# Two transformer blocks on one core: compressor MLP in column groups, squares on ScalarE, adds to GpSimd, a new planned order

## The chip, the core and the metric

The kernel runs on one core of a Trainium2 chip. The core has TensorE (PE, with its weight loads as PEld), VectorE (DVE), ScalarE (ACT), GpSimd (POOL) and SyncE (SP), which issues the transfers. The metric is the device time of one execution in microseconds (us).

## The reference, cut to what matters

All data is float32, one sequence of 512 tokens, 1024 features. Two blocks follow each other; the second has two layers, and most of the changed code lies there.

```python
def compress(t, j):                       # second block, sparse attention: 31 windows of 32 tokens
    z = (t[:, blk] + cmp_pos[j]).reshape(B, n_cmp, CMP_BLOCK * HD)   # 31 x 2048
    return jax.nn.silu(z @ cmp_w1[j]) @ cmp_w2[j]                    # 2048 x 128, then 128 x 64

# linear attention, per head of 32 key features, chunks of 64 tokens
att = jnp.einsum('bhntd,bhnsd->bhnts', q * jnp.exp(b - b_mid), k * jnp.exp(b_mid - b))

for l in range(DEPTH):
    mod = cond @ w_mod[l] + b_mod[l]                    # six modulation vectors a layer
    ...
    x = x + gt1 * rms_norm(y, norm_g[l, 1])
    h = rms_norm(x, norm_g[l, 2]) * (1.0 + sc2) + sh2
    y = jnp.square(jax.nn.relu(h @ w_up[l])) @ w_down[l]   # 1024 -> 4096 -> 1024
    x = x + gt2 * rms_norm(y, norm_g[l, 3])
```

## The kernel before

Activations lie feature by feature on the 128 partitions. Every large product is made of three float32r products: a tensor is split into a rounded part `hi` (a copy on ScalarE) and a rest `lo` (a subtraction on VectorE), and `mm3` multiplies hi by hi, hi by lo and lo by hi. Weights come in blocks of 128x1024 (`raw`), are split into `wh`, and feed PE. From its third block of columns on, the up projection of the MLP is done by a scheme with seven products in place of eight (`winograd_fm`); its sums and differences of weight blocks are the tiles `w`.

The code writes no order. Each call on an engine is recorded in a `Plan`, with a cost in us and the buffers it touches. `schedule` then simulates the engines and picks, step by step, the ready instruction that can start first, and among those the one with the highest priority; the priority comes from due times counted backwards along PE's work and from a table `SCHED` by phase of the program (`bias` shifts a phase's priority, `wins` says how far ahead of the oldest open instruction a phase may take buffers). The resulting order is fixed in the program. Every instruction is emitted from one line (553 before, 558 after), so all rows of the profile carry that line, and instructions are told apart by their tiles: `pg` are the work tiles, `sa` and `sb` small columns, `ps` the PSUM banks, `xT` the residual, `mc` the modulation columns.

An addition written as `G.tensor_tensor` (G is GpSimd) is recorded for VectorE, and may be moved to GpSimd when `other[1] * fill <= free`: `other[1]` is its cost there, `free` the VectorE work that the planner sees at hand which does not need the second SBUF read path. With `fill = 1e9` none is moved. `op.port` marks the instructions that need that path: a GpSimd operation, or a VectorE one with two SBUF inputs.

The places touched: `mod_cols` makes eight of the 128 modulation sums of a row at a time; `attn_half` and `nsa_chain` hold the two softmax attentions; `nsa_chain` also holds the compressor MLP, whose 32 products a layer have 31 columns of weights each; `gla_chain` the linear attention; `ev_up` and `ev_quarter` the squared ReLU. At three places, which I call **crossings**, one product ends, the residual is normed, and the next product starts on the normed residual: `Sandwich.sums` and `Sandwich.apply`, whose inner loop is

```python
V.tensor_mul(self.gy[k][:, sl], self.gy[k][:, sl], bc1[:, :256])
G.tensor_tensor(xT[k][:, sl], xT[k][:, sl], self.gy[k][:, sl], op=OP.add)
```

followed by `make_h`, which reads `xT`. Each crossing does it for two halves of 256 tokens, eight tiles each.

Of the kernel before, what the change touches and what calls it, by code (L numbers as in the profile page):

```python
# [10 lines left out]
F32 = mybir.dt.float32  # L11
# [20 lines left out]
    ahead=3.0, alap=1.0, lead={'mods': 20}, near=0.0, rate=270000.0, stretch=1.0, slack={"pg": 4, "w4": 0},  # L32
    wins={
# [117 lines left out]
class Plan:  # L151
# [15 lines left out]
    rate = 3.1e5  # L167
    lead = {}
    share = True
    fill = 1e9  # L170

    def __init__(self, nc, pools, win=6000, slack=None, fifo=(), **kw):
        self.__dict__.update(kw)
# [2391 lines left out]
```

## Time and profile before

| | |
|---|---|
| median of 3 runs | 1946.89 us (1945.47 to 1948.85) |
| profiled execution, its own time | 1957.53 us |
| its span, first to last instruction | 1955.6 us |
| PE busy | 1878.0 us |
| DVE busy | 1651.0 us |
| ACT busy | 986.9 us |
| POOL busy | 12.6 us |
| mean granted clock of PE | 0.967 |

The profiled execution is 10.6 us longer than the median of the runs. Busy time of PE counts every matmul to its modelled end, so a busy PE can still have small gaps. A granted clock of 1.00 is 2.4 GHz, 0.50 is 1.2 GHz; a value between them is a mean over a stretch.

### The profile page before, as it was taken

To read this page: it belongs to the slowest core of one execution; us is meant where nothing else is said; L and a number is where in the kernel's file an instruction comes from. 1 tells how busy PE (TensorE), PEld (TensorE's weight loads), DVE (VectorE), ACT (ScalarE), POOL (GpSimd) and SP (SyncE) were. 2 spreads that over 40 slices of the span, in tenths; PEclk is the share of its full clock that TensorE was granted. 3 is DMA by queue.
4 is the path that set the end of the run, shared out by engine and by line. 5 is a ranking of instruction groups with operands and counts; after the bars stand their busy time and mean duration, and the time that the engine had idled before them with its cause. 6 is when DMAs were issued, how large, how long until landed. Compare 5 with 4: busy or idle time off the path is not lost.

```text
span 1955.6 us, 33131 instructions
## 1 busy us (share of the span) xinstructions
PE 1878.0 (96%) x12451; PEld 1680.7 (86%) x12451; DVE 1651.0 (84%) x3712; ACT 986.9 (50%) x1958; POOL 12.6 (1%) x29
## 2 busy tenths in 40 slices
PE   8889999999999999999889999989999989999998
PEld 3789887998898988778778899988987889999998
DVE  6978898897996879877999877797966789887777
ACT  4756675544334556545554444355753447433344
POOL 0000000000000000000000000001000000000000
PEclk9999999999999999979999999989998789999999
DMA  8633533337433156211245422414521023332221
GB/s 274 223 111 135 178 123 115 120 126 264 150 112 110 59 192 198 73 33 65 98 162 201 144 97 98 153 49 180 185 106 44 33 76 109 119 108 87 98 98 66
DMA packets 88240, 243.17 MB, mean 124 GB/s; under 512 B 10059, under 2 KB 27247, under 8 KB 87824
## 3 DMA queue, kind: packets, MB, share of 16 engines
q1 hardware_dynamic: 88080, 241.05, 36.3%
q8 instruction: 98, 1.61, 0.3%
q14 instruction: 62, 0.51, 0.1%
HBM read 232.63 MB, written 8.39 MB: 123 GB/s over the span
## 4 chain that ended last, share of the span: by engine, by line
PE 80%; DVE 16%; ACT 2%; issue 1%; DMA 1%; SPq 0%; DVEq 0%; ACTq 0%
PE ps L553 80%; DVE pg L553 10%; DVE sa L553 2%; ACT pg L553 1%; DVE wh L553 1%; DVE mraw L553 1%; DVE xT L553 1%; SPq L553 0%; DVE w L553 0%; ACT wh L553 0%; DMA pg<-in_hy_w_dram 0%; DMA gq<-in_k_norm_g_dram 0%; DMA kf<-pg 0%; DVE sb L553 0%; ACT mraw L553 0%
## 5 line engine op out<-in xcount | busy, mean ns | idle before, releaser
L553 PE MATMUL ps<-pg,wh 128*128 128x256 f32 (+1 forms) x6336 | 1102.3, 330 | 15.8 <-DVE pg L553 8.7
L553 PEld LDWEIGHTS ps<-pg,wh 128*128 128x128 f32 x6336 | 926.6, 191 | 122.7 <-issue 10.8
L553 PE MATMUL ps<-wh,pg 128*128 128x256 f32 (+2 forms) x2976 | 386.7, 285 | 9.8 <-ACT pg L553 5.2
L553 DVE TENSOR_TENSOR pg<-pg 128x256 f32<-128x256 f32 (+4 forms) x757 | 361.0, 512 | 32.4 <-ACT pg L553 19.2
L553 PEld LDWEIGHTS ps<-wh,pg 128*128 128x128 f32 x2976 | 370.1, 191 | 14.9 <-ACT pg L553 9.7
L553 ACT ACTIVATE wh<-raw 128x1024 fp32r<-128x1024 f32 (+3 forms) x280 | 257.8, 924 | 217.9 <-PE ps L553 209.9
L553 DVE TENSOR_TENSOR wh<-raw,wh 128x1024 fp32r<-128x1024 f32 (+3 forms) x280 | 294.1, 1053 | 66.8 <-ACT wh L553 51.8
L553 ACT ACTIVATE pg<-pg 128x256 fp32r<-128x256 f32 (+5 forms) x424 | 201.9, 500 | 201.9 <-DVE pg L553 159.9
L553 PE MATMUL ps<-pg 128*128 128x256 f32 (+9 forms) x1776 | 285.9, 311 | 14.1 <-DVE pg L553 6.0
L553 PEld LDWEIGHTS ps<-pg 128*128 128x128 f32 (+5 forms) x1776 | 240.6, 194 | 51.3 <-issue 13.9
L553 DVE TENSOR_TENSOR pg<-pg,ps 128x256 f32<-128x256 f32 (+1 forms) x428 | 192.8, 465 | 42.2 <-PE ps L553 33.2
L553 DVE TENSOR_TENSOR pg<-ps,pg 128x512 f32<-128x512 f32 (+7 forms) x274 | 146.2, 566 | 32.0 <-ACT pg L553 18.4
L553 ACT ACTIVATE pg<-ps 128x512 fp32r<-128x512 f32 (+5 forms) x214 | 106.2, 521 | 121.4 <-PE ps L553 104.3
L553 ACT COPY pg<-ps 128x256 f32<-128x256 f32 (+4 forms) x188 | 81.2, 449 | 107.6 <-PE ps L553 79.9
L553 ACT ACTIVATE wh<-w 128x512 fp32r<-128x512 f32 x112 | 70.2, 630 | 122.5 <-PE ps L553 67.8
L553 DVE TENSOR_TENSOR wh<-w,wh 128x512 fp32r<-128x512 f32 x112 | 76.9, 686 | 30.3 <-PE ps L553 18.1
L553 DVE CUSTOM_DVE_ANT_0 mraw<-mraw,crow 128x1024 f32<-128x1024 f32 x72 | 87.4, 1220 | 7.6 <-DMA mraw<-in_wmT_dram 7.6
L553 PE MATMUL ps<-ident,pg 128*128 128x128 f32 (+1 forms) x513 | 84.9, 279 | 4.6 <-DVE pg L553 3.7
L553 ACT ACTIVATE mraw<-mraw 128x1024 f32<-128x1024 f32 x56 | 59.3, 1060 | 55.4 <-DVE mraw L553 55.2
L553 PEld LDWEIGHTS ps<-ident,pg 128*128 128x128 f32 (+1 forms) x513 | 62.4, 144 | 16.2 <-DVE pg L553 3.5
L553 ACT ACTIVATE pg<-ps,sa 128x512 f32<-128x512 f32 (+3 forms) x112 | 60.3, 549 | 27.1 <-DVE sa L553 23.6
L553 DVE TENSOR_TENSOR mraw<-mraw,crow 128x1024 f32<-128x1024 f32 x56 | 68.0, 1219 | 0.8 <-DMA mraw<-in_wmT_dram 0.8
(135 smaller groups left out, 1144.4 us busy)
## 6 DMA issues: line engine op xcount, KB each, us to landing
mraw<-in_wmT_dram SPq DMA_DIRECT2D x128, 512.0 KB, 4.1
raw<-in_w_up_dram SPq DMA_DIRECT2D x64, 512.0 KB, 3.2
raw<-in_w_down_dram SPq DMA_DIRECT2D x64, 512.0 KB, 3.3
raw<-in_w_in_dram SPq DMA_DIRECT2D x32, 512.0 KB, 4.1
raw<-in_od_w_in_dram SPq DMA_DIRECT2D x28, 512.0 KB, 3.4
raw<-in_ev_w_in_dram SPq DMA_DIRECT2D x20, 512.0 KB, 3.5
raw<-in_w_dram SPq DMA_DIRECT2D x16, 512.0 KB, 5.0
raw<-in_w_o_dram SPq DMA_DIRECT2D x16, 512.0 KB, 3.2
```

What stands on the lines that cost most here:

```text
L553: o.fn(*[r(v) for v in o.args], **{k: r(v) for k, v in o.kw.items()})
```

## The change

Seven edits. The compressor MLP's products go to four groups of 32 columns of the PE array (two for each of keys and values), and the halves are added afterwards. The linear attention's products alternate between two heads. The squared ReLU is a Relu and two Squares on ScalarE, where one Square writes the rounded part. The modulation sums are all done by the fused VectorE operation. One of two softmax scalings goes to ScalarE. `fill` becomes 0.5, the port rule looks at the inputs by position, and the table `SCHED` has new numbers (two lines stand for it).

```diff
-        "L0 gemm 0": -8, "L0 gemm 2": -8, "L0norm": -100, "L0out": -207, "L0q": 151, "L1 gemm 0": 145,
+        "": -15, "L0 gemm 0": -8, "L0 gemm 2": -8, "L0norm": 20, "L0out": -215, "L0q": 106, "L1 gemm 0": 145,
...
+    fill=0.5, ahead=3.0, near=0.0,
...
-        big = [v for v in ins if max(v.shape[1:], default=1) > 1]
+        big = [v for v in list(a)[0 if "out" in k else 1:] + [v for n, v in k.items() if n not in ("out", "accum_out")]
+               if isinstance(v, View) and max(v.shape[1:], default=1) > 1]
...
+                if not f:
+                    op.cost *= 0.25 if w == 31 else 0.5 if a[1].shape[0] <= 64 else 0.7 if w == 64 else 1.0
...
-            if t in ((1, 2, 4, 5, 7) if i < 4 else (2, 5, 7)):
-                G.tensor_tensor(raw, raw, crow, op=OP.mult)
-                A.activation(raw, raw, AF.Copy, accum_out=dst[:, t:t + 1])
-            else:
-                V.tensor_tensor_reduce(raw, raw, crow, 1.0, 0.0, OP.mult, OP.add, accum_out=dst[:, t:t + 1])
+            V.tensor_tensor_reduce(raw, raw, crow, 1.0, 0.0, OP.mult, OP.add, accum_out=dst[:, t:t + 1])
...
-            V.tensor_scalar(pr, pr, rz, None, op0=OP.mult)
+            A.activation(pr, pr, AF.Copy, scale=rz)
...
+        for q in range(4):
+            wq = [pg(), pg()]
+            for j in range(2):
+                D_(wq[j], a["cmp_w1_2"][l, j, q])
+            for i0 in (0, 2):
+                for j in range(2):
+                    zv = zst[j].rearrange("p (b n e) -> p b n e", b=2, n=32)
+                    for i in (i0, i0 + 1):
+                        g = 32 * (2 * j + i - i0)
+                        ab, pe = divmod(q * 4 + i, 8)
+                        T.matmul(ph[g:g + 31, 0:P], zv[:, ab, ab:ab + 31, pe], wq[j][:, i * P:(i + 1) * P],
+                                 start=(q + i0 == 0), stop=(q == 3 and i0 == 2), tile_position=(0, g),
+                                 skip_group_check=True)
+        yield
+        hs, hb = pg(), hp()
         for j in range(2):
...
+            A.copy(hb[0:31, j * P:j * P + P], ph[64 * j + 32:64 * j + 63, 0:P])
+            V.tensor_add(hs[0:31, j * P:j * P + P], ph[64 * j:64 * j + 31, 0:P], hb[0:31, j * P:j * P + P])
+        A.activation(hs[0:31, 0:256], hs[0:31, 0:256], AF.Silu)
...
-                        for b in range(2):
-                            V.tensor_scalar(pt[b], pt[b], rz[:, b:b + 1], None, op0=OP.mult)
+                        V.tensor_scalar(pt[0], pt[0], rz[:, 0:1], None, op0=OP.mult)
+                        A.activation(pt[1], pt[1], AF.Copy, scale=rz[:, 1:2])
...
-            for h in (2 * pr, 2 * pr + 1):
-                ps = axt()
-                for tt in range(4):
+            heads = {h: axt() for h in (2 * pr, 2 * pr + 1)}
+            for tt in range(4):
+                for h, ps in heads.items():
...
         def ev_up(m, ps):
-            r, f = pg(), pg()
+            r, f, hi, lo = pg(), pg(), pg(F32R), pg(F32R)
             A.activation(r, ps, AF.Relu)
-            V.tensor_mul(f, r, ps)
-            hid.append(split(f, eng=G))
+            A.activation(f, r, AF.Square)
+            A.activation(hi, r, AF.Square)
+            V.tensor_sub(lo, f, hi.bitcast(F32))
+            hid.append((hi, lo))
...
-                            V.scalar_tensor_tensor(f, src, 0.0, src, op0=OP.max, op1=OP.mult)
-                        split(f, eng=G, hi=tiles[m][0][:, sl], lo=tiles[m][1][:, sl])
+                        A.activation(r, src, AF.Relu)
+                        A.activation(hi, r, AF.Square)
+                        A.activation(f, r, AF.Square)
+                        V.tensor_sub(lo, f, hi.bitcast(F32))
```

What the planner makes of it, at three places. The first is PE at the compressor of the second block's first layer (31x128 are its products, `wh` x 272 those of the linear attention's projection, `ident` transposes). Before:

```order
L553 MATMUL ps<-wh_377,pg 128x272
L553 MATMUL ps<-pg 31x128
L553 MATMUL ps<-ident,pg 128x128 x4
L553 MATMUL ps<-pg 31x128 x5
L553 MATMUL ps<-ident,pg 128x128 x4
L553 MATMUL ps<-pg 31x128 x17
L553 MATMUL ps<-ident,pg 128x128 x4
L553 MATMUL ps<-pg 31x128 x3
L553 MATMUL ps<-ident,pg 128x128 x4
L553 MATMUL ps<-pg 31x128 x6
L553 MATMUL ps<-wh_375,pg 128x272
```

After:

```order
L558 MATMUL ps<-wh_378,pg 128x272
L558 MATMUL ps<-wh_377,pg 128x272
L558 MATMUL ps<-pg 31x128 x32
L558 MATMUL ps<-wh_375,pg 128x272
L558 MATMUL ps<-wh_376,pg 128x272
```

The 32 products stand in one piece, and the transposes between them went elsewhere.

The second is VectorE in the first half of the first crossing, where the projection `w_o` ends and the MLP begins (`mc_409` are the modulation columns). Before:

```order
L553 SCALAR_TENSOR_TENSOR sa<-sa 128x2
L553 SCALAR_TENSOR_TENSOR pg<-ps,mc_409,xT 128x256
L553 TENSOR_TENSOR pg<-pg,ps 128x256 x2
L553 TENSOR_TENSOR xT<-xT,pg 128x256
L553 TENSOR_TENSOR pg<-pg,ps 128x256
L553 TENSOR_TENSOR xT<-xT,pg 128x256
L553 TENSOR_TENSOR pg<-pg,ps 128x256
L553 SCALAR_TENSOR_TENSOR pg<-xT,mc_409,ps 128x256
```

After:

```order
L558 SCALAR_TENSOR_TENSOR sa<-sa 128x2
L558 TENSOR_TENSOR pg<-pg,ps 128x256 x4
L558 SCALAR_TENSOR_TENSOR pg<-xT,mc_409,ps 128x256
L558 TENSOR_TENSOR pg<-pg,ps 128x256
L558 SCALAR_TENSOR_TENSOR pg<-xT,mc_409,ps 128x256
L558 TENSOR_TENSOR pg<-pg,ps 128x256
L558 SCALAR_TENSOR_TENSOR pg<-xT,mc_409,ps 128x256
```

The additions into `xT` are gone from VectorE. They stand on GpSimd, which before has only copies and memsets in this part of the program; after, its rows here are (the rows ahead of the first `xT` belong to the chains before the crossing, the `xT` rows to its two halves):

```order
L558 COPY pg<-pg 128x4x64 x8
L558 TENSOR_TENSOR pg<-pg,msk 128x256 x5
L558 TENSOR_TENSOR pg<-pg 128x512 x8
L558 TENSOR_TENSOR pg<-pg 128x256 x2
L558 TENSOR_TENSOR xT<-xT,pg 128x256 x8
L558 TENSOR_TENSOR pg<-pg 128x256
L558 TENSOR_TENSOR xT<-xT,pg 128x256 x7
```

Of the 16 additions of this crossing, 15 moved to GpSimd. The third place is ScalarE in the up projection of the first layer's MLP (`wh<-raw` and `wh<-w` are splits of weights, `pg<-pg 128x256` the squared ReLU and its split, `mraw` a modulation sum). Before:

```order
L553 ACTIVATE wh_373<-raw_370 128x1024
L553 ACTIVATE pg<-ps 128x256
L553 ACTIVATE wh_375<-raw_368 128x1024
L553 ACTIVATE pg<-pg 128x256
L553 ACTIVATE mraw_380,m_1_402<-mraw_380 128x1024
L553 ACTIVATE wh_377<-raw_369 128x1024
L553 ACTIVATE pg<-pg 128x256
```

After:

```order
L558 ACTIVATE wh_373<-raw_370 128x1024
L558 ACTIVATE pg<-ps 128x256
L558 ACTIVATE wh_375<-raw_368 128x1024
L558 ACTIVATE pg<-pg 128x256 x2
L558 ACTIVATE wh_377<-raw_369 128x1024
L558 ACTIVATE pg<-pg 128x256 x6
```

Between the same weight splits stand eight squares and ReLUs where two stood, and no modulation sum.

## Rows read from the trace of the kernel before

**Rows 1.** The page, busy time of PE and DVE: us, share, instructions.
```profile
PE 1878.0 (96%) x12451; PEld 1680.7 (86%) x12451; DVE 1651.0 (84%) x3712; ACT 986.9 (50%) x1958; POOL 12.6 (1%) x29
```

**Rows 2.** Windows by stage: stretch, length, busy of each engine, granted clock, DMA share, GB/s.
```profile
0.00:150.00 150.00, 129.15 (x791) 96.71 (x792) 119.23 (x294) 87.76 (x190) 0.77 (x10) 0.95 0.62 198
...
232.00:312.00 80.00, 74.00 (x442) 63.77 (x440) 77.12 (x169) 52.11 (x123) 0.00 (x0) 0.98 0.40 138
...
830.00:885.00 55.00, 54.70 (x291) 43.02 (x291) 41.32 (x102) 22.32 (x43) 0.00 (x0) 0.81 0.12 39
885.00:960.00 75.00, 65.06 (x444) 60.20 (x443) 65.58 (x185) 40.54 (x80) 0.00 (x0) 0.93 0.21 71
960.00:1060.00 100.00, 92.78 (x573) 82.85 (x572) 98.43 (x181) 53.21 (x95) 0.00 (x0) 0.95 0.50 169
...
1290.00:1335.00 45.00, 33.94 (x208) 31.64 (x207) 44.50 (x153) 25.45 (x61) 0.00 (x0) 0.77 0.17 58
...
1500.00:1535.00 35.00, 35.00 (x157) 28.62 (x157) 19.98 (x56) 7.17 (x13) 0.00 (x0) 0.61 0.04 16
1535.00:1608.00 73.00, 65.05 (x402) 58.05 (x401) 64.09 (x176) 33.98 (x65) 0.00 (x0) 0.88 0.20 70
1608.00:1915.00 307.00, 307.00 (x2605) 307.00 (x2605) 257.92 (x525) 137.66 (x257) 0.00 (x0) 1.00 0.29 101
1915.00:1955.60 40.60, 31.62 (x273) 31.41 (x271) 31.11 (x104) 18.62 (x56) 0.00 (x0) 0.93 0.18 66
```

**Rows 3.** The chain that ended last, in the second crossing, 1290 to 1335 us.
```profile
by line: DVE pg L553 48.1%; PE ps L553 13.7%; DVE xT L553 10.2%; DVE sa L553 9.5%; DVE wh L553 7.8%; ACT pg L553 5.5%; issue 4.9%; DVE sb L553 1.2%; DVEq L553 0.0%
```

**Rows 4.** Groups on PE by form: count, busy us, mean ns, idle before.
```profile
L553 PE MATMUL ps<-pg 128*31 128x128 f32 x128 | 16.4, 277 | 0.0
...
L553 PE MATMUL ps<-pg 32*128 32x128 f32 x64 | 9.5, 327 | 0.0
```

**Rows 5.** Timeline of PE from 720 us: start, length, matmul records.
```profile
720.66 0.31 PE L553 MATMUL ps<-sb,pg 128*64 128x31 f32 x4
720.90 0.32 PE L553 MATMUL ps<-pg,sb 128*31 128x64 f32 x8
```

**Rows 6.** Groups on VectorE by form.
```profile
L553 DVE TENSOR_TENSOR pg<-pg,ps 128x256 f32<-128x256 f32 x344 | 136.5, 413 | 30.2 <-PE ps L553 23.5 <-ACT pg L553 6.6
L553 DVE TENSOR_TENSOR pg<-pg 128x512 f32<-128x512 f32 x159 | 105.8, 683 | 4.3 <-ACT pg L553 3.2 <-DMA kf<-pg 0.8
...
L553 DVE CUSTOM_DVE_ANT_0 mraw<-mraw,crow 128x1024 f32<-128x1024 f32 x72 | 87.4, 1220 | 7.6 <-DMA mraw<-in_wmT_dram 7.6
...
L553 DVE TENSOR_TENSOR mraw<-mraw,crow 128x1024 f32<-128x1024 f32 x56 | 68.0, 1219 | 0.8 <-DMA mraw<-in_wmT_dram 0.8
...
L553 DVE SCALAR_TENSOR_TENSOR pg<-pg 128x256 f32<-128x256 f32 x90 | 36.5, 418 | 0.8
...
L553 DVE TENSOR_TENSOR xT<-xT,pg 128x256 f32<-128x256 f32 x48 | 19.8, 414 | 0.0
...
L553 DVE TENSOR_SCALAR pg<-pg,sa 128x512 f32<-128x512 f32 x40 | 18.7, 479 | 0.7
```

**Rows 7.** Groups on ScalarE by form.
```profile
L553 ACT ACTIVATE mraw<-mraw 128x1024 f32<-128x1024 f32 x56 | 59.3, 1060 | 55.4 <-DVE mraw L553 55.2
...
L553 ACT ACTIVATE pg<-pg 128x256 f32<-128x256 f32 x74 | 29.4, 413 | 25.6 <-DVE pg L553 19.3 <-DVE sa L553 5.9
...
L553 ACT ACTIVATE pg<-pg,sa 128x256 f32<-128x256 f32 x7 | 3.2, 497 | 2.2 <-DVE sa L553 2.2
```

**Rows 8.** Timeline of POOL from 1350 us.
```profile
1352.68 0.40 POOL L553 COPY pg<-pg 128x256 f32<-128x256 f32 x1 [161.69 <-ACT pg L553]
1353.75 3.07 POOL L553 COPY pg<-pg 128x256 f32<-128x256 f32 x3 [0.68 <-PE ps L553]
```

**Rows 9.** Timeline of VectorE in the same stretch.
```profile
1353.86 1.36 DVE L553 CUSTOM_DVE_ANT_0 mraw<-mraw,crow 128x1024 f32<-128x1024 f32 x1
...
1355.16 1.40 DVE L553 CUSTOM_DVE_ANT_0 mraw<-mraw,crow 128x1024 f32<-128x1024 f32 x1
```

More of the change, by code (lines that the diff above doesn't have):

```diff
@@ L31 @@
 SCHED = dict(
-    ahead=3.0, alap=1.0, lead={'mods': 20}, near=0.0, rate=270000.0, stretch=1.0, slack={"pg": 4, "w4": 0},
+    alap=1.0, lead={'mods': 20}, rate=270000.0, stretch=1.0, slack={"pg": 4, "w4": 0},
+    fill=0.5, ahead=3.0, near=0.0,
     wins={
[19 rows of a table removed]
[19 rows of a table added]
     },
     bias={
-        "L0 gemm 0": -8, "L0 gemm 2": -8, "L0norm": -100, "L0out": -207, "L0q": 151, "L1 gemm 0": 145,
-        "L1 gemm 1": 30, "L1f": 90, "L1norm": 270, "L1out": 23, "end": 170, "finN": 37, "gla 1": -15,
-        "gla chain 0": -92, "gla chain 1": -38, "gmlp 1": -8, "gmlp chain 1": -200, "head 0": 15,
-        "head 4": 15, "hyena chain 0": 223, "hyena chain 2": 90, "mlp 1": -253, "mods": -15, "nsa 0": 8,
-        "sand1 0": 30, "sand2 0": 210, "wo 0": -315, "wo 1": -228,
+        "": -15, "L0 gemm 0": -8, "L0 gemm 2": -8, "L0norm": 20, "L0out": -215, "L0q": 106, "L1 gemm 0": 145,
+        "L1 gemm 1": 30, "L1f": 98, "L1norm": 270, "L1out": -7, "end": 170, "finN": 37, "gla 1": -15,
+        "gla chain 0": -32, "gla chain 1": -38, "gmlp 0": -15, "gmlp 1": -8, "gmlp chain 0": -30,
+        "gmlp chain 1": -80, "head 0": 75, "head 4": 15, "hyena chain 0": 321, "hyena chain 1": 60,
+        "hyena chain 2": 90, "mlp 1": -253, "mods": -45, "nsa 0": 8, "sand1 1": 8, "sand2 0": 210,
+        "wo 1": -228,
     },
@@ L169 @@
     share = True
-    fill = 1e9
+    fill = 1.0
     def __init__(self, nc, pools, win=6000, slack=None, fifo=(), **kw):
@@ L1969, in nsa_chain @@
         ph = axt()
-        for j in range(2):
-            zv = zst[j].rearrange("p (b n e) -> p b n e", b=2, n=32)
-            for q in range(4):
-                wq = pg()
-                D_(wq, a["cmp_w1_2"][l, j, q])
-                for i in range(4):
-                    pa = q * 4 + i
-                    ab, pe = divmod(pa, 8)
-                    T.matmul(ph[0:31, j * P:j * P + P], zv[:, ab, ab:ab + 31, pe], wq[:, i * P:(i + 1) * P],
-                             start=(pa == 0), stop=(pa == 15))
-        yield
-        hs = pg()
-        A.activation(hs[0:31, 0:256], ph[0:31, 0:256], AF.Silu)
+        for q in range(4):
[13 more added lines that the diff above has]
+        hs, hb = pg(), hp()
+        for j in range(2):
+            A.copy(hb[0:31, j * P:j * P + P], ph[64 * j + 32:64 * j + 63, 0:P])
+            V.tensor_add(hs[0:31, j * P:j * P + P], ph[64 * j:64 * j + 31, 0:P], hb[0:31, j * P:j * P + P])
+        A.activation(hs[0:31, 0:256], hs[0:31, 0:256], AF.Silu)
         w2 = pg()
@@ L2193, in gla_chain @@
                              tile_position=(32 * h, 0))
+            for h, ps in heads.items():
                 t = pg()
@@ L2412, in ev_quarter @@
                     def ev_quarter(m, q, src):
-                        f, sl = hp(), HV[q]
-                        if m + q == 0:
-                            A.activation(f, src, AF.Relu)
-                            V.tensor_mul(f, f, src)
-                        else:
-                            V.scalar_tensor_tensor(f, src, 0.0, src, op0=OP.max, op1=OP.mult)
-                        split(f, eng=G, hi=tiles[m][0][:, sl], lo=tiles[m][1][:, sl])
+                        r, f, sl = hp(), hp(), HV[q]
+                        hi, lo = tiles[m][0][:, sl], tiles[m][1][:, sl]
+                        A.activation(r, src, AF.Relu)
+                        A.activation(hi, r, AF.Square)
+                        A.activation(f, r, AF.Square)
+                        V.tensor_sub(lo, f, hi.bitcast(F32))
                     winograd_fm(wu, c0 * P + b * 256, act, diff, ev_quarter)
```

38 rows, old and new, of the table wins are left out of this document.

## The prediction

> **What bounds the kernel now.** I read the page first, for the busy shares: PE is busy for 1878 of 1955.6 us, VectorE for 1651, ScalarE for 987 [rows 1]. So no change of the other engines can give more than the 78 us in which PE is idle, plus what PE loses by running slowly; only a change of PE's own work goes beyond that. Then I cut the span into stages, to see where the idle time lies and who fills the stage [rows 2]. In the last long stage, 1608 to 1915 us, PE is busy throughout, at full clock, 2605 products at 0.118 us each: there VectorE has 49 us to spare and nothing done to it can help. The idle time sits in six places: 20.9 us in the first 150, 6.0 from 232 to 312, 7.2 from 960 to 1060, 9.0 behind 1915, and in the three crossings, 885 to 960, 1290 to 1335 and 1535 to 1608, 9.9, 11.1 and 8.0 us. In the crossings VectorE is busy for 65.6 of 75, 44.5 of 45 and 64.1 of 73 us. The chain of waits inside the second crossing says the same from the other side: VectorE has over three quarters of it, 10.2% with `xT` as output, and PE 13.7% [rows 3].
>
> The clock is the second loss. In a crossing with a granted 0.77 over 45 us, PE was at 1.2 GHz for 45 x 0.23 x 2 = 20.7 us; the same sum gives 10.5 us for the first, 17.5 for the third and 10 for 960 to 1060 [rows 2]. There PE had stood idle before the clock fell. In 830 to 885 and 1500 to 1535, the linear attention, it had not: PE is busy for 54.7 of 55 and 35 of 35 us, and yet at 1.2 GHz for 20.9 and 27.3 us, while it ran products that fill a small part of the array. Those two I take as unchanged.
>
> **The change, part by part.** Instructions are counted in the two built programs; durations are busy time over count.
>
> *Compressor.* Before, 64 products (128 records, two each) take 16.4 us, 0.128 a record, one after the other [rows 4]. Whether four column groups run side by side, another part of the same chain shows: four products with 31 columns of weights into four partition groups, 8 records of 64 columns, last 0.32 us together, with a tail of one product in it [rows 5]. At half the width they would have needed 8 x 0.064 = 0.51 us in turn and then the tail. I take full overlap: 128 records / 4 x 0.11 = 3.5 us, a gain of **12.9 us**. Bounds: 0 if they don't overlap here, 12.9. The two small copies and two sums per layer that join the halves lie in a chain beside 272-wide products, and cost nothing while PE has those; without them they would put some 1.2 us a layer between the products and the SiLU.
>
> *Linear attention heads.* 9.5 us for 32 products [rows 4]. Taking turns can at best halve it (4.7), and before the planner had already mixed some heads, so I take **3 us**; bounds 0 and 4.7.
>
> *Additions to GpSimd.* 177 additions leave VectorE, 80 of them 512 wide, 97 up to 256. At 0.665 and 0.413 us [rows 6] that is 53 + 40 = 93 us of VectorE's time. The trace of before has no addition on GpSimd. The nearest row is a copy of 256 elements, 0.40 us alone [rows 8], one input in place of two: so 0.40 to 0.80 for a narrow addition, 0.75 to 1.5 for a wide one. I take the middle, 0.6 and 1.1, 146 us in all, for two inputs need more reads than one but the fixed part doesn't double. The copies also show a trap: three that started beside VectorE sums with two SBUF inputs took 3.07 us in place of 1.2, and those sums 1.36 and 1.40 in place of 1.22 [rows 6, 8, 9]. The two engines hold each other up there. Where the additions went decides: 44 are the `xT` sums of the crossings, beside VectorE work that reads PSUM, which needs no second read path; 25 or so stand in the first 150 us.
>
> The rule of the Trainium skill that speaks against this edit is in GPSIMD Engine Reference, section Engine selection: elementwise additions belong on VectorE, GpSimd is about 2x slower with two inputs. By its ratio (1.96) my narrow addition would be 0.81 and the wide one 1.30, 183 us in all, an estimate from that page; no row here shows a two-input operation on GpSimd, and [rows 8, 9] agree with the contention that the page names.
>
> *Squared ReLU and softmax scaling.* VectorE loses 84 products of 256 at 0.406 (34 us), 28 that read PSUM at 0.397 (11 us), 8 wide ones (5 us), and 56 scalings, 32 of them at 0.468 and the rest shorter (some 22 us) [rows 6]. ScalarE gains 196 operations of 256 at 0.40 (78 us) and the scalings at 0.46 or more (some 28), and loses the 59.3 us of modulation sums [rows 7]: about 50 us more, 1037 in all. I cost that at nothing, since ScalarE is busy half the time and 25 of 45 us in the tightest crossing [rows 2]; if the cover fails, the next PSUM bank is late and PE pays each delay in full.
>
> *Modulation.* 56 multiplications at 1.21 us become 56 fused ones at 1.21 [rows 6]: nothing on VectorE, and a wait of ScalarE less.
>
> So VectorE falls from 1651 to about 1485 us. What that gives PE:
>
> *Crossings.* The `xT` sums were 10.2% of the chain over 45 us, 4.6 us; three crossings, **13.8 us**. All 44 sums are 18.2 us, the upper bound; the lower one is the second rival. What comes late next is the chain of splits that follows, and GpSimd itself: eight sums at 0.6 are 4.8 us, while VectorE's two remaining operations on eight tiles need 6.5 or more, so VectorE sets the pace.
>
> *The other VectorE stages* (first 150, 232 to 312, 960 to 1060): 34.1 us idle, some 7 of them the first loads. A third of the rest, **9 us**; bounds 0 and 18.
>
> *Clock.* 59 us at 1.2 GHz stand behind idle time (crossings and 960 to 1060); PE is busy for seven eighths of it, which costs 26 us. If the idle time halves I take a third of that back, **8 us**; bounds 0 and 20.
>
> Sum: 12.9 + 3 + 13.8 + 9 + 8 = 46.7. The profiled execution's own time is 1957.5 us, so 1910.8 there; it stands 10.6 us above the median of the runs, so I predict **1900 us** (1946.9 - 46.7).
>
> The new priorities move everything else, and no row of before prices that. In the stages where PE is full they can cost nothing but a stall of PE, and the order shows the same instructions there.
>
> **Rivals.**
>
> *Only PE's own part is real.* The planner spends the freed VectorE time elsewhere, the crossings wait for the next engine. For it: ScalarE and the small sums follow each other in the same chain (9.5% `sa`, 5.5% ACT) [rows 3]. Against it: VectorE is busy 44.5 of 45 us. Time: 1946.9 - 15.9 = 1931.
>
> *More comes back.* With VectorE 10% lighter, idle time in crossings and stages goes by the upper bounds, 12.9 + 4.7 + 18.2 + 18 + 20 = 74: 1873.
>
> *GpSimd stops VectorE.* The place is the first 150 us and the crossings. If a wide addition takes 1.5 us and a narrow one 0.8 and VectorE stands still meanwhile, 25 wide ones cost 25 x (1.5 - 0.67) = 21 us and 44 narrow ones 44 x (0.8 - 0.41) = 17, with no gain there and none of the clock: 38 - 16 = 22 us slower, 1969. It decides from 16 / 69 = 0.23 us lost per addition. For it: two held copies and two stretched sums [rows 8, 9]. Behind it stands the rule of the Trainium skill named above (GPSIMD Engine Reference, Engine selection). Against it: beside the `xT` sums VectorE reads PSUM.
>
> *The change does nothing that can be measured.* The column groups run in turn, as the bounds allow, and what VectorE gives is taken by waits for ScalarE: 1947.
>
> **How the numbers follow.** My forecast, 1885 to 1918, has 55%; more than it, 13%; PE's part alone, 14%; no effect, 7%; slower, 11%. A measurement of this kernel tells about 0.2% (4 us) from no change. Faster: 82% less the edge of the PE-only case, 80%; same 8%; slower 12%. The range is to leave out two in ten: from 1866, a little below the case of more relief, to 1945, which leaves out no effect and slower.
>
> **What would show it.** The 31-column records at about 0.03 us each; VectorE near 1485 us and ScalarE near 1040; idle time of PE in the crossings at half of 29 us or less, with a clock above 0.9; narrow GpSimd additions near 0.6 us where VectorE reads PSUM. I am wrong if VectorE's sums next to GpSimd's stretch beyond 0.41 and 0.67 us by about the time they were to save, or if ScalarE becomes what PE waits for in the crossings.

## The result, and the profile of the changed kernel

The changed kernel takes 1899.5 us (median of 4 runs, 1897.4 to 1903.4) where the kernel before takes 1946.2 on the same chip: a ratio of 0.976, with a 95% interval of 0.972 to 0.980. It is faster by 47 us. The profiled execution took 1898.6 us, with a span of 1896.8. That is 58.8 us less than the span of before; why this is more than 47 is a part of the answer below.

The page of the changed kernel, against [rows 1]:

```profile
PE 1834.3 (97%) x12451; PEld 1645.8 (87%) x12451; DVE 1542.9 (81%) x3419; ACT 1026.6 (54%) x2112; POOL 196.8 (10%) x206
```

PE is busy for 43.7 us less with the same number of instructions, and idle for 62.5 in place of 77.5 us. So three quarters of the difference are not idle time: either products that overlap, or products at a higher clock. VectorE lost 108 us, GpSimd got 184.

The windows by stage answer to [rows 2]. The columns are the stretch, its length, the busy time of PE, PEld, VectorE, ScalarE and GpSimd, the granted clock, DMA share and GB/s:

```profile
0.00:150.00 150.00, 130.65 (x820) 97.61 (x821) 117.52 (x276) 89.48 (x201) 31.99 (x35) 0.95 0.65 202
...
800.00:860.00 60.00, 55.63 (x332) 44.10 (x331) 48.15 (x120) 32.36 (x64) 10.38 (x10) 0.92 0.11 36
860.00:930.00 70.00, 66.32 (x447) 60.86 (x445) 59.72 (x164) 36.23 (x69) 15.43 (x19) 0.96 0.23 76
930.00:1030.00 100.00, 100.00 (x635) 90.66 (x636) 99.04 (x185) 67.62 (x134) 6.15 (x7) 0.99 0.53 174
...
1250.00:1290.00 40.00, 32.18 (x236) 29.86 (x235) 39.46 (x138) 23.70 (x56) 11.79 (x16) 0.91 0.22 71
1290.00:1450.00 160.00, 156.11 (x983) 133.62 (x982) 130.95 (x296) 97.38 (x206) 22.74 (x28) 0.98 0.42 142
...
1500.00:1570.00 70.00, 65.11 (x481) 62.63 (x480) 63.36 (x162) 42.98 (x87) 19.66 (x24) 0.93 0.23 76
1570.00:1860.00 290.00, 290.00 (x2470) 289.94 (x2469) 214.66 (x416) 152.28 (x321) 15.60 (x12) 1.00 0.32 104
```

The crossings, now at 860, 1250 and 1500 us, have 3.7, 7.8 and 4.9 us of idle time where they had 9.9, 11.1 and 8.0, and a clock of 0.96, 0.91 and 0.93 in place of 0.93, 0.77 and 0.88. The stage after the first one (930 to 1030) has none, where 7.2 stood. There is new idle time too, around the linear attention: 4.4 us in 800 to 860, 3.9 in 1290 to 1450 and 1.2 in 1450 to 1500, where before had 0.6 in all.

The forms on PE, against [rows 4]:

```profile
L558 PE MATMUL ps<-pg 32*128 32x128 f32 x64 | 10.2, 328 | 0.0
...
L558 PE MATMUL ps<-pg 128*31 128x128 f32 x128 | 4.6, 278 | 0.0
```

The compressor's records went from 16.4 to 4.6 us, 0.036 each; the heads of the linear attention, from 9.5 to 10.2, gained nothing.

The additions on GpSimd, for which before had no row, by form:

```profile
L558 POOL TENSOR_TENSOR pg<-pg 128x512 f32<-128x512 f32 x48 | 67.3, 1407 | 471.8 <-DVE pg L558 230.2 <-ACT pg L558 193.7 <-issue 45.3
L558 POOL TENSOR_TENSOR xT<-xT,pg 128x256 f32<-128x256 f32 x44 | 30.7, 740 | 40.5 <-DVE pg L558 40.5
L558 POOL TENSOR_TENSOR pg<-pg 128x256 f32<-128x256 f32 x24 | 20.7, 865 | 246.3 <-ACT pg L558 124.7 <-PE ps L558 68.7 <-DVE sa L558 22.5
...
L558 POOL TENSOR_TENSOR w<-raw,w 128x512 f32<-128x512 f32 x12 | 15.6, 1300 | 262.5 <-DVE w L558 255.1 <-DVE pg L558 7.4
```

A narrow one takes 0.74 to 0.87 us and a wide one 1.28 to 1.59, at the upper ends of the bounds (0.80 and 1.5) or above them. The sums beside them on VectorE, against [rows 6]:

```profile
L558 DVE CUSTOM_DVE_ANT_0 mraw<-mraw,crow 128x1024 f32<-128x1024 f32 x128 | 155.4, 1220 | 8.5 <-DMA mraw<-in_wmT_dram 5.5 <-ACT crow L558 3.0
L558 DVE TENSOR_TENSOR pg<-pg 128x256 f32<-128x256 f32 x250 | 100.5, 428 | 12.6 <-ACT pg L558 9.7 <-DMA pg<-in_hy_w_dram 1.6 <-POOL pg L558 0.6
L558 DVE TENSOR_TENSOR pg<-pg 128x512 f32<-128x512 f32 x111 | 78.0, 712 | 3.0 <-ACT pg L558 2.1
```

They are hardly longer than before: 712 ns for 683 where they are 512 wide, and the long modulation sums not at all.

**Where the time went.** Every kernel here puts out the same 3,659,980 columns of products. So I add up, record by record, the columns that PE has put out, and ask when each kernel has got as far as the changed one has at a given moment. The difference grows where a kernel loses. (In us; the columns are points in time of the changed kernel; the order of the work differs a little between kernels that are planned apart, so single steps are good to some us.)

```
changed kernel at        300    700    830    930   1030   1250   1320   1450   1500   1570   1894
before                  +0.8   +3.7   +8.0  +21.1  +32.3  +32.3  +45.7  +42.6  +57.3  +58.8  +59.6
one column group        -2.1   -2.2   +2.7   +2.6   +2.5   +2.5   +6.9   +3.7   +3.1   +2.6   +3.0
no cost factors         +0.3   +0.3   +7.3   +7.8   +7.1   +7.1  +10.5   +7.7  +12.0  +11.4  +11.0
old table               -2.4   -0.6   -0.6  +11.2  +18.9  +19.7  +19.1  +18.2  +23.5  +22.2  +22.1
no sharing              +8.9  +12.2  +16.6  +19.6  +20.0  +20.0  +27.6  +22.8  +40.0  +41.3  +41.2
old conflict rule      +14.2  +19.6  +21.1  +21.3  +31.6  +31.8  +36.0  +37.4  +38.4  +39.1  +39.9
square, planned anew    -0.9   -0.8   -0.6   -0.2   +0.7   +2.0   +2.2   +1.3  +15.2  +14.8  +16.4
```

Before loses 17.4 us between 700 and 930 (compressor, linear attention, first crossing), 11.2 in the stage behind it, 13.4 around the second crossing with the second compressor, 14.7 in the second linear attention, and in the two MLPs, 1030 to 1250 and behind 1570, next to nothing. The rows follow single, profiled executions. These were longer than the median of their runs by about 11 us for before, 8 for the old table, 6 for no sharing and 10 for the square planned anew, and 4 shorter for one column group and no cost factors.

### The profile page after: what moved, and what is told of

Same layout as the page of the kernel before. It is cut to its first block, busy times and chain, and to the rows that moved or that the text cites. A ratio compares the mean times of both kernels' runs of the same rounds, so it can differ in the third digit from the quotient of the medians.

```text
span 1896.8 us, 33344 instructions
## 1 busy us (share of the span) xinstructions
PE 1834.3 (97%) x12451; PEld 1645.8 (87%) x12451; DVE 1542.9 (81%) x3419; ACT 1026.6 (54%) x2112; POOL 196.8 (10%) x206
## 4 chain that ended last, share of the span: by engine, by line
PE 83%; DVE 12%; ACT 2%; issue 2%; DMA 1%; POOL 0%; SPq 0%; DVEq 0%; ACTq 0%
PE ps L558 83%; DVE pg L558 7%; DVE sa L558 2%; ACT pg L558 2%; DVE wh L558 1%; DVE mraw L558 1%; ACT wh L558 0%; DMA raw<-in_w_dram 0%; DVE w L558 0%; POOL xT L558 0%; DMA vec<-in_vec_dram 0%; DVE xT L558 0%; SPq L558 0%; DVE sb L558 0%; ACT L558 0%
## 5 line engine op out<-in xcount | busy, mean ns | idle before, releaser
L558 DVE TENSOR_TENSOR pg<-pg 128x256 f32<-128x256 f32 (+4 forms) x656 | 317.5, 516 | 45.4 <-ACT pg L558 35.7
L558 ACT ACTIVATE pg<-pg 128x256 f32<-128x256 f32 (+5 forms) x630 | 274.0, 472 | 143.3 <-DVE pg L558 81.1
L558 PE MATMUL ps<-pg 128*128 128x256 f32 (+9 forms) x1776 | 264.6, 303 | 9.5 <-DVE pg L558 3.6
L558 PEld LDWEIGHTS ps<-pg 128*128 128x128 f32 (+5 forms) x1776 | 225.6, 188 | 43.5 <-issue 16.5
L558 DVE TENSOR_TENSOR pg<-pg,ps 128x256 f32<-128x256 f32 (+1 forms) x392 | 174.8, 465 | 59.6 <-PE ps L558 55.7
L558 POOL TENSOR_TENSOR pg<-pg 128x512 f32<-128x512 f32 (+4 forms) x101 | 120.7, 1202 | 858.0 <-ACT pg L558 434.6
L558 DVE TENSOR_TENSOR pg<-ps,pg 128x512 fp32r<-128x512 f32 (+8 forms) x278 | 146.4, 561 | 42.1 <-ACT pg L558 27.3
L558 DVE CUSTOM_DVE_ANT_0 mraw<-mraw,crow 128x1024 f32<-128x1024 f32 x128 | 155.4, 1220 | 8.5 <-DMA mraw<-in_wmT_dram 5.5
L558 ACT ACTIVATE pg<-ps 128x512 fp32r<-128x512 f32 (+4 forms) x212 | 105.0, 523 | 100.1 <-PE ps L558 80.0
L558 DVE TENSOR_REDUCE sa<-ps 128x1 f32<-128x512 f32 (+4 forms) x96 | 51.2, 571 | 11.4 <-PE ps L558 11.1
```

Of the source, the lines that this page charges most:

```text
L558: o.fn(*[r(v) for v in o.args], **{k: r(v) for k, v in o.kw.items()})
```

## The experiments

All times are medians; ratios are to the kernel before on the same chip, with 95% intervals. The changed kernel stands at 0.976.

**1. The additions back on VectorE, same order.** The planner plans as before, but what it gave to GpSimd is sent to VectorE:

```diff
-                (o.fn, o.cost), o.eng, o.other = o.other, e, None
+                o.cost, o.eng, o.other = o.other[1], e, None
```

> The changed kernel with the 177 additions back on VectorE, each at the very place of the order where GpSimd had it; nothing else moves. They cost VectorE about 93 x 0.43 + 80 x 0.71 = 97 us. Theory A (GpSimd takes a load off VectorE that PE feels in the crossings): most of the 12.6 us of idle time that the three crossings lost comes back, and some low clock with it: 1915 to 1930 us. Rival B (the additions are worth nothing; the squared ReLU and the scalings on ScalarE relieve VectorE): 1896 to 1904 us. Rival C (GpSimd holds VectorE up more than it takes from it): faster, 1880 to 1895 us.

Measured: 1932.2 us, ratio 0.991 (0.988 to 0.995), 30 to 33 us slower; theory A, a little beyond its upper end. PE's waits that end with a work tile of VectorE grew from 13.0 to 22.5 us, its whole idle time from 62.5 to 76.4, and its time at 1.2 GHz from 68.5 to 89.6. Since PE's order is the same record for record, the loss can be placed product by product: 7.2 us in the first 150, then 5.3, 3.8 and 3.3 in the three crossings, 4.1 in 930 to 1030, 4.4 in 1290 to 1370, and 2.7 in 400 to 500. The places are those the prediction named, and the crossings sum to 12.4.

**2. The compressor in one column group, same order.** The four sums lie in one bank beside each other, so the compressor's output is not the reference's.

```diff
-                        T.matmul(ph[g:g + 31, 0:P], zv[:, ab, ab:ab + 31, pe], wq[j][:, i * P:(i + 1) * P],
-                                 start=(q + i0 == 0), stop=(q == 3 and i0 == 2), tile_position=(0, g),
+                        T.matmul(ph[0:31, 4 * g:4 * g + P], zv[:, ab, ab:ab + 31, pe], wq[j][:, i * P:(i + 1) * P],
+                                 start=(q + i0 == 0), stop=(q == 3 and i0 == 2), tile_position=(0, 0),
```

> The changed kernel with all 64 products of the compressor in the first column group, into four areas of columns of the same bank, in the same order on every engine. Theory A (the four groups run side by side, and PE is the bound there): the 31-column records go from 4.6 back to about 16.4 us, and the kernel is 11 to 13 us slower, 1910 to 1913 us. Rival B (PE's saving is lost in a wait of what follows, the copies and sums that join the halves): the records grow the same, the kernel by less than 5 us.

Measured: 1905.5 us, ratio 0.978 (0.974 to 0.982), 4 to 6 us slower. The form on PE:

```profile
L558 PE MATMUL ps<-pg 128*31 128x128 f32 x128 | 14.8, 274 | 0.0
```

The records grew by 10.2 us. By products, the loss is 4.9 us at the first compressor and 4.1 at the second, 9.0 together, and nothing behind them gave it back. In other places this execution was at 1.2 GHz for 48.7 us where the changed kernel's was for 68.5, which hides 6 of the 9. Theory A in kind; the size falls between the two.

**3. Without the cost factors, planned anew.** The change also has a line that lowers the planner's cost of thin products. Here it is gone.

```diff
-                if not f:
-                    op.cost *= 0.25 if w == 31 else 0.5 if a[1].shape[0] <= 64 else 0.7 if w == 64 else 1.0
```

> The changed kernel without the line that lowers the planner's cost of thin products (0.25, 0.5, 0.7); the order is planned anew with it. Theory A (the lower costs make the planner spread the thin products of the linear attention among dense ones, which keeps the granted clock up there): the time at 1.2 GHz goes from 68 us back to over 110, most of it in the linear attention, and the kernel takes 1915 to 1930 us. Rival B (the clock there stays up through the heads in turn or the priorities): less than 80 us at 1.2 GHz, 1895 to 1908 us.

Measured: 1914.4 us, ratio 0.983 (0.978 to 0.988), 14 us slower, but only 58.5 us at 1.2 GHz. My theory A of the clock fell; rival B's clock was right and its time was not. By products the loss lies at 700 to 830, at the second compressor and in the second linear attention, where the thin products are. The compressor's records take 5.7 us here, and PE is idle for 70.9 us in place of 62.5. The factors earn their time by a better order, not by the clock.

**4. The table of before.** Windows and biases as they were, sharing and the cost factors kept.

> The changed kernel with the windows and biases of before, and the new rule for the additions on GpSimd kept; all edits of the operations stay. Theory A (the edits carry the gain, the table adjusts them): 1903 to 1918 us, the idle time of the crossings below 25 us, the 31-column records at about 5 us. Rival B (the new table carries the gain): 1930 us or more, with the idle time of before in the crossings or the low clock of before in the linear attention.

Measured: 1912.7 us, ratio 0.983 (0.978 to 0.988), 13 us slower: theory A's time, with rival B's clock. Two windows in the linear attention (of the profiled execution, 1920.8 us, the slowest of four):

```profile
840.00:871.00 31.00, 31.00 (x130) 24.14 (x131) 19.43 (x54) 11.09 (x20) 7.17 (x7) 0.50 0.00 1
1464.00:1482.00 18.00, 18.00 (x60) 11.43 (x60) 6.53 (x14) 6.57 (x14) 0.00 (x0) 0.53 0.09 30
```

PE has no idle microsecond there and runs at 1.2 GHz, as in [rows 2]. I counted the time at 1.2 GHz between the first and the last thin product of the first linear attention in every profile of this study. With the old table (five profiles) it is 15.0 to 20.9 us; with the new one (nine) it is 0, and 6.8 in the kernel without sharing. So there the clock goes with the order that the table makes. In the changed kernel some low time, 10.2 us from 851 on, still follows, but behind a wait of PE for VectorE, which its timeline shows:

```profile
852.54 3.12 PE L558 MATMUL ps<-ones,pg 128*128 128x1 f32 x14 [4.25 <-DVE sa L558]
```

**5. The changed kernel once more.**

> The changed kernel once more, nothing edited, as the measure for its neighbours. The run with one column group was at 1.2 GHz for 48.7 us where the changed kernel was for 68.5. Theory A (which stretches fall to the low clock differs between executions of one kernel): the low-clock time of this execution differs from 68.5 us by more than 10. Rival B (the order of the products sets it): 65 to 72 us again. Time in both: 1897 to 1905 us.

Measured: 1898.5 us, ratio 0.977 (0.974 to 0.980), 66.5 us at 1.2 GHz: rival B for this pair. Up to 1030 us every stage runs within 0.2 us of the first execution. The stretch into and through the second linear attention, 1370 to 1500, differs most, by 1.7 us; experiment 12 shows a larger difference there.

**6. No sharing, planned anew.** `fill=1e9`, so that no addition goes to GpSimd.

> The changed kernel with the rule that lets the planner place additions on GpSimd set so high that it never does; the order is planned anew, so that the planner knows of the full VectorE. Theory A (the load itself is what the crossings feel): VectorE near 1600 us, idle time of PE in the three crossings 25 us or more, 1918 to 1935 us. Rival B (the run with the additions put back lost its time because its order was made for GpSimd): 1900 to 1912 us.

Measured: 1932.5 us, ratio 0.994 (0.991 to 0.996), 34 us slower. Theory A, though the idle time of the crossings, 20.3 us, comes to less than I said. VectorE is busy for 1596.1 us. That the order was planned for it changes nothing: 1932 us here and in experiment 1. Its windows:

```profile
0.00:150.00 150.00, 124.32 (x706) 88.92 (x707) 113.84 (x269) 81.05 (x164) 0.77 (x10) 0.90 0.63 198
880.00:945.00 65.00, 61.55 (x421) 56.55 (x420) 56.13 (x152) 33.05 (x62) 0.00 (x0) 0.97 0.21 68
...
1275.00:1325.00 50.00, 38.41 (x244) 35.26 (x245) 49.03 (x165) 27.47 (x65) 0.00 (x0) 0.83 0.18 60
...
1480.00:1530.00 50.00, 45.10 (x206) 36.55 (x205) 32.99 (x91) 13.22 (x23) 0.00 (x0) 0.66 0.04 11
1530.00:1600.00 70.00, 64.75 (x444) 60.28 (x443) 59.98 (x167) 34.56 (x68) 0.00 (x0) 0.93 0.23 76
```

All the other edits together are worth 14 us without sharing, 1946.5 to 1932.5. Where both sides have sharing and the new rule they are worth 36, 1935.4 (experiment 10) to 1899.5.

**7. Before with sharing.** One number, `fill=0.5`, in the kernel before.

> The kernel before with one number more: the planner may place additions on GpSimd (fill 0.5); all else as it was, planned anew. Theory A (this carries most of the gain by itself): 20 to 32 us faster than before, 1916 to 1928 us, with VectorE down by 100 us or so. Rival B (GpSimd pays only once the squared ReLU and the scalings have left VectorE, or with the new table): within 10 us of before.

Measured: 1962.2 us, ratio 1.009 (1.006 to 1.012): 16 to 17 us slower than before. Both theories missed. What happened stands in the forms on GpSimd and on VectorE, and at 246 us in their timelines:

```profile
L553 POOL TENSOR_TENSOR pg<-pg 128x256 fp32r<-128x256 f32 x63 | 67.4, 1074 | 334.4 <-ACT pg L553 332.0 <-issue 2.4
L553 POOL TENSOR_TENSOR mraw<-mraw,crow 128x1024 f32<-128x1024 f32 x20 | 55.8, 2790 | 204.0 <-DMA mraw<-in_wmT_dram 204.0
...
L553 POOL TENSOR_TENSOR w<-raw 128x512 f32<-128x512 f32 x15 | 31.9, 2125 | 37.7 <-DMA raw<-in_w_up_dram 15.5 <-issue 12.2 <-DVE wh L553 10.1
```

```profile
L553 DVE TENSOR_TENSOR pg<-pg,ps 128x256 f32<-128x256 f32 x344 | 137.2, 416 | 40.9 <-PE ps L553 33.0 <-ACT pg L553 4.5 <-POOL pg L553 1.2
L553 DVE TENSOR_TENSOR pg<-pg 128x256 f32<-128x256 f32 x233 | 103.4, 470 | 13.6 <-ACT pg L553 7.2 <-DMA pg<-in_hy_w_dram 6.0
L553 DVE CUSTOM_DVE_ANT_0 mraw<-mraw,crow 128x1024 f32<-128x1024 f32 x72 | 101.8, 1416 | 11.9 <-DMA mraw<-in_wmT_dram 11.8
```

```profile
246.32 3.30 POOL L553 TENSOR_TENSOR mraw<-mraw,crow 128x1024 f32<-128x1024 f32 x1 [0.87 <-DMA mraw<-in_wmT_dram]
```

```profile
248.05 2.66 DVE L553 CUSTOM_DVE_ANT_0 mraw<-mraw,crow 128x1024 f32<-128x1024 f32 x1
```

A VectorE sum of 1.22 us takes 2.66 beside a GpSimd multiplication. It is the holding of [rows 8, 9], all over the kernel, and it meets the sums with both inputs in SBUF. Record by record, the 25 fused modulation sums that an operation of GpSimd overlapped lasted 1.79 us on average, the 47 others 1.22. Of the narrow sums (`pg<-pg`, 256 wide) 49 overlapped ones lasted 0.67, the 184 others 0.42; the wide ones 0.97 (19) and 0.69 (81). Of the narrow sums that read PSUM (`pg<-pg,ps`) 170 were overlapped, and all lasted 0.42.

**8. Before with the compressor of the changed kernel.** Nothing else.

> The kernel before with the compressor of the changed one and nothing else, planned anew with the old costs. Theory A (PE is the bound where the compressor stands): the 31-column records go from 16.4 to about 4.6 us and the kernel is 8 to 13 us faster, 1934 to 1941 us. Rival B (the saving goes into waits behind it): within 4 us of before, with the records as short.

Measured: 1942.6 us, ratio 0.998 (0.996 to 1.000), 4 us faster by the medians, rival B by its time; the interval reaches to no change. The planner of before has other products between, here transposes, so that the records shrink to 7.2 us and not to 4.6:

```profile
L553 PE MATMUL ps<-pg 128*31 128x128 f32 x128 | 7.2, 285 | 0.0
```

```profile
708.10 0.65 PE L553 MATMUL ps<-pg 128*31 128x128 f32 x10
708.69 0.66 PE L553 MATMUL ps<-ident,pg 128*128 128x128 f32 x4
709.27 1.31 PE L553 MATMUL ps<-pg 128*31 128x128 f32 x34
711.70 0.66 PE L553 MATMUL ps<-ident,pg 128*128 128x128 f32 x4 [1.12 <-POOL pg L553]
```

A row of 34 records takes 0.039 us each, one of ten 0.065.

**9. The changed kernel with the old conflict rule.** The change also has a new rule by which the planner tells which VectorE operations conflict with GpSimd: it counts every large input, also one that the operation writes back to.

```diff
-        big = [v for v in list(a)[0 if "out" in k else 1:] + [v for n, v in k.items() if n not in ("out", "accum_out")]
-               if isinstance(v, View) and max(v.shape[1:], default=1) > 1]
+        big = [v for v in ins if max(v.shape[1:], default=1) > 1]
```

> The changed kernel with the planner's old rule for which VectorE operations it takes to conflict with GpSimd (the old one leaves out the input that an operation also writes); sharing, table and edits stay, planned anew. Putting additions on GpSimd made the changed kernel faster by 34 us and the kernel before slower by 16. Theory A (the rule makes the difference: without it additions are put beside VectorE operations that they hold up): more additions on GpSimd, VectorE's two-input sums longer than in the changed kernel, 1915 to 1935 us. Rival B (the edits that relieve VectorE and the table make it): 1897 to 1908 us.

Measured: 1937.3 us, ratio 0.995 (0.992 to 0.998), 38 us slower: theory A, a little beyond its range. It is no better than no sharing at all. Forms on VectorE, where the means stand at 1319, 448 and 737 for 1220, 428 and 712:

```profile
L557 DVE CUSTOM_DVE_ANT_0 mraw<-mraw,crow 128x1024 f32<-128x1024 f32 x128 | 167.9, 1319 | 6.0 <-DMA mraw<-in_wmT_dram 3.3 <-ACT crow L557 2.4
...
L557 DVE TENSOR_TENSOR pg<-pg 128x256 f32<-128x256 f32 x237 | 100.1, 448 | 13.9 <-ACT pg L557 11.7 <-DMA pg<-in_hy_w_dram 1.2 <-PE ps L557 0.3
...
L557 DVE TENSOR_TENSOR pg<-pg 128x512 f32<-128x512 f32 x95 | 68.9, 737 | 2.7 <-ACT pg L557 1.8
```

**10. Before with sharing and the new rule.** `fill=0.5` and the rule of experiment 9, the other way round.

> The kernel before with the additions shared (fill 0.5) and with the new conflict rule, nothing else, planned anew. Theory A (the rule decides): 20 to 35 us faster than before, 1912 to 1927 us. Rival B (GpSimd's multiplications for the modulation, 2.79 us each, and its longer work in the MLP are what costs, rule or none): 1940 to 1965 us.

Measured: 1935.4 us, ratio 0.993 (0.990 to 0.996). It is 12 to 14 us faster than before, between my two theories, and 27 us (by the medians) to 32 (by the ratios) faster than sharing without the rule.

From the four kernels with sharing I worked out what an addition on GpSimd costs VectorE. For each form of VectorE's records I take the number that left, at the mean they had without sharing (experiment 6 for the changed kernel, before for before), and by how much the records that stayed grew over that mean:

```
                              additions    their time     the rest     lost per    time against the
                              on GpSimd    on VectorE    grew by      addition    same without sharing
changed kernel                   177         96 us        11.5 us      0.065 us        -34 us
before, sharing, new rule        241        132 us        51   us      0.21  us        -14 us
changed kernel, old rule         230        127 us        55   us      0.24  us         +5 us
before, sharing, old rule        295        166 us        95   us      0.32  us        +17 us
```

The new rule keeps the additions away from the sums that are held up. Of the three forms with both inputs in SBUF that experiment 7 names, GpSimd overlaps 40 records in the changed kernel and 58 in this one; with the old rule it is 92 and 93. The sums with PSUM as an input are overlapped in all four, at no cost: in the changed kernel 95 of them, with a mean of 411 ns for 414.

**11. The second square on VectorE, same order.** The Square that writes `f` is sent as a multiplication to VectorE, at its place.

```diff
             A.activation(f, r, AF.Square)
+            pl.ops[-1].ret = True
...
+            if hasattr(o, "ret"):
+                self.engs["DVE"].real.tensor_mul(r(o.args[0]), r(o.args[1]), r(o.args[1]))
+                continue
```

> The changed kernel with the second square of the squared ReLU on VectorE, at the very place of the order where ScalarE had it; nothing else moves. Theory A (the work of the MLP lies where PE is full at full clock and VectorE has time to spare): VectorE goes up by 40 to 90 us, ScalarE down by as much, the kernel by less than 5 us, and that in the third crossing. Rival B (this relief is a main part of the gain): 10 us or more slower.

Measured: 1920.7 us, ratio 0.986 (0.980 to 0.992), about 20 us slower; theory A fell. By products, 13.3 us are lost in 930 to 1250 and 7.9 behind 1570. Two windows:

```profile
1030.00:1260.00 230.00, 226.43 (x1414) 199.51 (x1414) 184.36 (x344) 102.94 (x199) 8.62 (x8) 1.00 0.38 125
...
1590.00:1880.00 290.00, 287.33 (x2411) 284.65 (x2410) 225.47 (x452) 132.67 (x258) 15.57 (x12) 1.00 0.30 100
```

PE's idle time grew by 3.6 and 2.7 us in these two and by 3.0 in the stage ahead, 9 of the 21 us, and most of its waits there end with VectorE; the rest, with the clock at 1.00, hides in records that start later one after the other and still count as busy. VectorE has time to spare, 65 of 290 us, and yet is late.

**12. The squared ReLU of before, planned anew.** So that the order is made for it.

```diff
-            r, f, hi, lo = pg(), pg(), pg(F32R), pg(F32R)
+            r, f = pg(), pg()
             A.activation(r, ps, AF.Relu)
-            A.activation(f, r, AF.Square)
-            A.activation(hi, r, AF.Square)
-            V.tensor_sub(lo, f, hi.bitcast(F32))
-            hid.append((hi, lo))
+            V.tensor_mul(f, r, ps)
+            hid.append(split(f, eng=G))
```

and `ev_quarter` as it was.

> The changed kernel with the squared ReLU of before (its multiplication on VectorE), planned anew, so that the order is made for it. The second square put on VectorE in the changed kernel's own order cost 21 us, most of it in the two MLPs, where PE shows hardly any idle time. Theory A (VectorE's work itself is what the MLPs feel, whatever the order): 1912 to 1925 us, with the loss between 930 and 1250 and behind 1570 us. Rival B (it was the order, made for ScalarE; planned anew the MLPs run as before): 1896 to 1907 us.

Measured: 1905.0 us, ratio 0.981 (0.977 to 0.984), 6 to 8 us slower. In the MLPs it loses 1.3 us in 1030 to 1250 and 1.6 behind 1570: rival B. What the profiled execution (1914.9 us, the slowest of its four) loses beyond that lies in one place, the second linear attention, 13.9 us. There the PE records from 1432 to 1515 us, 398 of them in a row, have the forms of those that the changed kernel runs from 1430 to 1500, in the same order: 82.9 us for 70.0. A window of each, this kernel first, the changed kernel second:

```profile
1472.00:1494.00 22.00, 22.00 (x87) 17.89 (x88) 9.82 (x37) 3.51 (x6) 1.27 (x1) 0.53 0.01 1
```

```profile
1450.00:1472.00 22.00, 22.00 (x142) 15.51 (x140) 11.10 (x29) 8.90 (x18) 0.00 (x0) 0.97 0.14 48
```

37.5 us at 1.2 GHz in the one, 6.8 in the other. They are two programs, and the other engines' work differs between them. But this kernel's own runs differ too: the mean granted clock was 0.976 in the profiled one and 0.979 to 0.984 in the three shorter ones. The same holds for before against experiment 8: 296 records in the same order, 64.6 us with 32.3 at 1.2 GHz in the profile of before, 53.4 us with 5.9 in the other, whose window answers to the row at 1500 us in [rows 2]:

```profile
1485.00:1520.00 35.00, 35.00 (x220) 26.51 (x218) 23.92 (x69) 12.52 (x24) 0.00 (x0) 1.00 0.09 31
```

## Why the prediction was right, step by step

The time, 1900 us, and the main reasons held. The profiled executions close like this, in us gained: compressor's records 11.8, heads -0.7, idle time of the crossings 12.6, other idle time that went 11.2, clock 31.3 (half of 62.6 us less at 1.2 GHz, 131.1 to 68.5, with PE taken as busy in them), new idle time around the linear attention -8.9. That is 57.3 of 58.8. Of the clock, 20.5 us of low time, and so 10.2 us, stand in the second linear attention, where experiments 8 and 12 show that executions with the same order on PE differ. Without it 47 us remain, which is what the medians say. The granted clocks of the runs fit that. The kernel before was run 63 times beside the experiments: its median clock is 0.974, where its profiled execution had 0.967. For ten runs of the changed kernel it is 0.983. At the medians the share below full clock, times the span, is 51 us for the one and 32 for the other, so the clock gives back some 18 us and not 31.

That the prediction's sum was also 46.7 is luck: its parts are others, and what it put too high (compressor, heads) and what it left out (the new idle time) cancel against a clock that gave back more than twice the 8 us:

- *Compressor, 12.9.* Right in kind. The records take 11.8 us less. In the same order the gain is 9.0 by products (experiment 2); alone in the kernel before it is some 4 us, not clear of no change (8), where the planner leaves transposes between the groups' products.
- *Linear attention heads, 3.* Wrong: 9.5 became 10.2, and 9.3 in the second execution. No gain that a record shows; no run has this edit alone.
- *Crossings, 13.8.* Right: 12.6 of idle time, 12.4 by products when the additions go back (1). That the next engine would take it all (1931) did not come true.
- *Other VectorE stages, 9.* Right in sum: 7.2 us behind the first crossing, 1.5 in the first 150, and 2.5 behind that (6.0 in 232 to 312, now 3.5 in 150 to 300). The first 150 us are worth more than that reading shows: there sharing alone carries 7 us (1) to 14 (6), and other edits take most of it away, for before is only 0.8 us behind at 300 us.
- *Clock, 8.* Mis-sized, by the step "Those two I take as unchanged". The first linear attention and what follows it went from 20.5 us at 1.2 GHz to 10.2, worth 5; old and new table part there (4). The second, 27.3 to 6.8, differs between executions with one order on PE (8, 12). The rest, 62.6 - 10.3 - 20.5 = 31.8 us, lies in the crossings and the stage behind the first, and is worth 15.9, twice the forecast but inside its bounds, all by these two profiles. My first explanation, that the new cost factors keep the clock up, fell (3).
- *Additions to GpSimd, 0.6 and 1.1.* Too low: 0.74 to 0.87 and 1.28 to 1.59. GpSimd worked for 184 us more, not 146. The Trainium skill's page GPSIMD Engine Reference, section Engine selection, puts two-input operations there at about twice VectorE's time, an estimate of 183 us in the prediction. The rows agree, with 1407 ns against 687 on VectorE without sharing (2.0) and 740 against 414 (1.8).
- *VectorE at 1485.* Too low, by 58 us. The other edits brought it from 1651 to 1596 (6), 55 us for the 72 of the sum, and sharing to 1543, 53 for 93. The records' own lengths fell by 85 us with sharing, 96 less the 11.5 by which the others grew; busy time fell by less, as the records of VectorE overlap.
- *GpSimd stops VectorE, decided at 0.23 us lost per addition.* The mechanism is right, and the number fits by luck. In the prediction 0.23 is what PE's own gain of 16 us leaves to each of 69 additions, against before. What I measured is VectorE's loss over all 177 to 295 additions, against the same kernel without sharing: there 0.065 and 0.21 are faster, 0.24 is about even, 0.32 is slower. What keeps this kernel under it is the conflict rule, which stood in the diff and which I did not price; with the old one sharing costs 17 us in the kernel before, as the rival said (7), and gains nothing in the changed one (9).
- *Squared ReLU at nothing.* Right for the MLPs once the order is made for it (12: about 3 us), wrong where it isn't (11). "Nothing done to it can help" holds for less work on VectorE; it does not say that work can be added there at no cost.
- *The new priorities.* I said that no row prices them. The table is worth 13 us (4) and the cost factors 14 (3), each with the other kept.

What stays open: how the 14 us of the other edits without sharing split, and why they and sharing give more together (47) than apart (14 without sharing, 12 to 14 for sharing with the rule alone). The heads in turn, the scalings and the modulation were not tried alone.

## What to carry to other kernels

Work that moves to an engine that holds up its neighbour pays by where it lands: count what the neighbour's remaining records lose per moved operation before counting what it is spared. An edit that is made in a frozen order and one that is planned anew answer different questions; the first gives the place of a loss, the second its price. And before a low clock is explained by an order of instructions, look for the same order in a second execution.

## What the runs showed of the hardware

The granted clock isn't settled by the program. In the 63 runs of the kernel before the mean lay between 0.964 and 0.980, and the time goes with it: the ten runs at 0.964 to 0.967 took 1955 to 1962 us, the 26 at 0.976 to 0.980 took 1936 to 1944. The kernel with one column group runs, up to its compressor near 700 us, the same instructions in the same order on every engine as the changed kernel; it was at 1.2 GHz there for 10.2 us, the changed kernel in both profiles for 20.5.

A low clock also comes without idle time of PE ahead of it. The 398 records of the second linear attention, whose idle time, at most 1.3 us, comes behind the fall of the clock, took 70.0 us in one profile and 82.9 in another, with 6.8 and 37.5 us at 1.2 GHz. What lets the clock fall there is not shown. The first linear attention, in contrast, is low in all five profiles with the old table.

One operation on GpSimd can more than double one on VectorE: a sum of 1.22 us took 2.66 beside a multiplication. What it meets are VectorE operations with both inputs in SBUF; sums that read PSUM kept their 0.41 to 0.42 us (7, 10). GpSimd is held up likewise. The `xT` sums of the changed kernel, beside VectorE work nearly all of which reads PSUM, took 721 to 757 ns each; in experiment 7, where some met other work, up to 1739.
